# One engine for the sums of the Strassen projections, and swapped PSUM pools

## The chip, the cores and the metric

The kernel runs on one core of a Trainium2 chip. The metric is the device time of one execution in microseconds (us). The engines are TensorE (PE, with its weight loads PEld), VectorE (DVE), ScalarE (ACT), GpSimd (POOL) and SyncE (SP, which here issues most DMA transfers). Matrix products accumulate in PSUM, which is split into eight banks; everything else lies in SBUF.

## The reference, cut to what matters

```python
for layer in range(2):
    if layer == 0:
        h = rms_norm(x, norm_even)
        a_u, a_z, q, k, v, b_z = split(h @ w_in_even)
        ya = s5_branch(a_u, ...) * silu(a_z)
        yb = retention_branch(q, k, v, gn_gain) * silu(b_z)
        x = x + concatenate([ya, yb]) @ w_out_even      # (1024 x 2048) @ (2048 x 1024): stage E
    else:
        h = rms_norm(x, norm_odd)
        p = h @ w_in_odd                                # u, v, z of 2048 columns each
        y = spatial_gating(gelu(u), gelu(v), ...) * silu(z)
        x = x + y @ w_out_odd                           # (1024 x 2048) @ (2048 x 1024): stage O
return rms_norm(x, final_norm)
```

The sequence has 1024 positions, the model 1024 channels, and everything is float32.

## The kernel before, in words

**Numbers.** A float32 product is made of three products of a shorter format. `split` (lines 64 to 66) makes the high half of a tile with a cast on ACT (L65, `whi` for weights, `yhi` for activations) and the low half with a subtraction on DVE (L66, `wlo`, `ylo`). `mm3` (L102 to L104) then issues high by high, low by high and high by low into one PSUM bank.

**Projections.** Both output projections, E after the even layer and O after the odd one, run through `strassen_out`, a seven-product scheme (Strassen and Winograd) over 2x2 blocks. Products p0 to p6 follow one another. Each has four quarters c0 to c3 of its inner dimension, and each quarter is 24 matmuls: 4 row blocks, 2 slices, 3 products of `mm3`. Between the products stand sums of blocks, a quarter at a time and 128x1024 in size: of weights `s1` = a21 + a22 (L1330), `s2` = s1 - a11 (through `vsub`), a12 - s2 for p3 (L1308) and a11 - a21 for p5 (L1312); of activations `t1`, `t2`, `t3` (through `vsub`) and `t4` (L1342). `sums(n)` places them a fixed number of quarters behind the start. `prep` makes the operands of a quarter, `evac` (L1354) adds a finished bank into an SBUF tile, p2 takes the banks of p1 again, p3 goes on accumulating on p2's sums and p4 to p6 on p0's, so that such a product's first matmul in a bank waits for the eviction of what stands there. Raw weights arrive in two pools, `raw` (two buffers) and `wr` (five buffers), all loaded from SP's queue in a chain (`load`, L1241).

**Before E** stands the last step of the attention: its output `on` is normalised on DVE (L1148) and transposed on PE into `ps_ot` (L1158). **The v units** of the retention projections (`quads_sums`, L785; rotary products L903 to L909) have four 256-column blocks of weights and the sums s1 (L793), s2 (L794), a11 - a21 (L795) and a12 - s2 (L1025). The same `quads_sums` also serves sv2, a later stage of the odd layer.

**Order.** Each engine executes its instructions in order. That order is made by a scheduler that simulates the time line, from the dependences and the order of the code. `tc.issue_after(x)` adds an edge that keeps an instruction behind x; the list `lastv` holds the last DVE operation of the chain, and `vsub` uses it. In `run_e` the pools of four PSUM banks each are handed over as `psAs`; p0 takes `psAs[False]`, and p1 to p3 take the other one. Banks become free in the order in which their former users finish.

In the trace, tiles named slS2h and slS2l (E) or slT1h and slT1l (O) hold s1 and s2; slB... and slT... hold activations and their sums, and slC... the results.

Of the kernel before, what the change touches and what calls it, by code (L numbers as in the profile page):

```python
# [14 lines left out]
MUL, ADD, SUB = ALU.mult, ALU.add, ALU.subtract  # L15
# [10 lines left out]
def tile_hybrid_trunk(ctx: ExitStack, tc: tile.TileContext, A, out, dbg=None):  # L26
    nc = tc.nc
# [36 lines left out]
    def split(hi, lo, src, E=nc.vector):  # L64
        nc.scalar.copy(hi, src)  # L65
        return E.tensor_tensor(lo, src, hi.bitcast(F32), SUB)  # L66
# [206 lines left out]
    with tc.tile_pool(name="s5p", bufs=1, reuse_waits="tile") as pp:  # L273
# [72 lines left out]
        V = nc.vector  # L346
# [436 lines left out]
            a = vq[k] = uw.tile([128, 4, 256], F32, tag="a2", name=f"a2{k}", bufs=2)  # L783
            ld(out=a, in_=wcols(w, c0 + 256, 256, 4 * k, 4))

    def quads_sums():
        i = done[0]
        done[0] += 2
        a11, a12, a21, a22 = raws[i], raws[i + 1], vq[0], vq[1]
        s1 = uw.tile([128, 4, 256], F32, tag="s14", name="s1")  # L790
        s2 = uw.tile([128, 4, 256], F32, tag="s23", name="s2")
        P = nc.gpsimd
        P.tensor_tensor(s1, a21, a22, ADD)  # L793
        P.tensor_tensor(s2, s1, a11, SUB)  # L794
        P.tensor_tensor(a21, a11, a21, SUB)  # L795
        return a11, a12, s2, a21, a22, s1

# [163 lines left out]
    for n, (nm, h) in enumerate(seqB):  # L961
        nn = seqB[n + 1][0] if n + 1 < len(seqB) else None
        V = nc.vector
        if nm != "v":
            t0, t1, t2, t3 = nxt
            nxt = []
            if n < NEARLY:
                cA = cE[n]
            else:
                cA = c_pair("q")  # L970
                first_two(t0, cA)
            cB = c_pair("k")
            c11, c12, c21, c22 = cA[:, 0], cA[:, 1], cB[:, 0], cB[:, 1]
            if nn in ("q", "k", "z"):
                w_pair_raw()
                src = w_pair()
                nxt.append(w_pair_split(src[0]) if n + 1 >= NEARLY else None)
            if n == 0:
                with tc.issue_after(loads[max(raws)].ins):
                    load_tab()  # L980
                    load_tab()
            if nn is None:
                pre = {(0, 0): prefetch(0, 0)}
                yr = load_y()
            p6 = prodB(half(t1, 0), T2)
            V.tensor_tensor(c12, p6, c12, ADD)
            p7 = prodB(half(t1, 1), T3)
            V.tensor_tensor(c22, p7, c12, ADD)
            if nn in ("q", "k", "z"):
                nxt.append(w_pair_split(src[1]))  # L990
            p4 = prodB(t3, T4)
            V.tensor_tensor(c21, p4, c22, ADD)
            rot(nm, h, 0, c11, c21)
            if nn == "v":
                quads_raw(w_in, 4096 + seqB[n + 1][1] * 512)
                nxt.append(split4(raws[done[0]]))
            p5 = prodB(half(t2, 0), T1)
            V.tensor_tensor(c22, p5, c22, ADD)
            V.tensor_tensor(c12, p5, c12, ADD)
            if nn == "v":  # L1000
                nxt.append(split4(raws[done[0] + 1]))
            p3 = prodB(half(t2, 1), Be[1, 1])
            V.tensor_tensor(c12, p3, c12, ADD)
            if nn == "v":
                qs = quads_sums()
                qt = split4(qs[2])
            with tc.issue_after(loads["s4"].ins) if nn == "v" else ExitStack():
                rot(nm, h, 1, c12, c22)
            if nn in ("q", "k", "z"):
                nxt += [w_pair_split(o) for o in src[2:]]  # L1010
            elif nn is None:
                w_split(done[0])
        else:
            def keep(c, t, q):
                ld(out=vv_d[4 * t:4 * t + 4, :, h * 512 + q * 256:h * 512 + (q + 1) * 256].rearrange("c p d -> p c d"), in_=c)

            a11, a12, s2, s3, a22, s1 = qs
            c11, c12 = c_pair("q", (4, 256)), c_pair("q", (4, 256))
            p1 = prod4(PB, "p", Be[0, 0], nxt[0])
            post(c12, p1, None)  # L1020
            p2 = prod4(PB, "p", Be[1, 0], nxt[1])
            post(c11, p2, c12)
            keep(c11, 0, 0)
            c21, c22 = c_pair("k", (4, 256)), c_pair("k", (4, 256))
            nc.gpsimd.tensor_tensor(a12, a12, s2, SUB)  # L1025
            t2 = qt
            t3 = split4(s3)
            p6 = prod4(PB, "p", T2, t2)
            post(c12, p6, c12)
            t4 = split4(a22)  # L1030
            p7 = prod4(PB, "p", T3, t3)
            post(c22, p7, c12)
            t5 = split4(s1)
            p4 = prod4(PB, "p", T4, t4)
            post(c21, p4, c22)
            keep(c21, 0, 1)
            t6 = split4(a12)
            w_pair_raw()
            src = w_pair()
            nxt = [w_pair_split(src[0])]  # L1040
            p5 = prod4(PB, "p", T1, t5)
            post(c22, p5, c22)
            keep(c22, 1, 1)
            post(c12, p5, c12)
            nxt.append(w_pair_split(src[1]))
            p3 = prod4(PB, "p", Be[1, 1], t6)
            post(c12, p3, c12)
            keep(c12, 1, 0)
            nxt += [w_pair_split(o) for o in src[2:]]
        if 2 <= n < 6:  # L1050
            y_transpose(2 * n - 4)
            y_transpose(2 * n - 3)
# [181 lines left out]
    def strassen_out(w, wk, ysrc, yt, s2t, ct, xsrc, fin, ysl, nfirst, tmp=None, late=False, pre=None):  # L1234
# [29 lines left out]
        def wl(d, q, c, own=False):  # L1264
            a = op.tile([128, 2, 512], F32, tag="wr", name="wr", bufs=5) if own else wraw_p.tile([128, 2, 512], F32, tag="raw", name="raw")
            loads["wl"] = load(a, wcols(w, d * 512, 512, wk[8 * q + 2 * c], 2))
            return a

        def ws(src):
            hi = wspl_p.tile([128, 2, 512], F32R, tag="whi", name="whi")  # L1270
            lo = wspl_p.tile([128, 2, 512], F32R, tag="wlo", name="wlo")
            lastv[:] = [split(hi, lo, src)]
            return hi, lo

        lastv = []

        def ys(src):
            p, th, tl, n = ysl(yn[0], op)
            yn[0] += 1
            hi = p.tile([128, 2, 512], F32R, tag=th, name="yhi", bufs=n)  # L1280
            lo = p.tile([128, 2, 512], F32R, tag=tl, name="ylo", bufs=n)
            lastv[:] = [split(hi, lo, src)]
            return hi, lo

        V, P = nc.vector, nc.gpsimd
        op, yn = None, [0]
        C, ops = {}, {}
        first = []
# [12 lines left out]
        def prep(p, c):  # L1301
            if p < 2:
                return ws(wl(0, p, c)), ys(yf(p, 0, c))
            if p == 2 or p == 4:
                return ws(s2(c)), ys(yf(0, 0, c))
            if p == 3:
                a12 = wl(0, 1, c)
                P.tensor_tensor(a12, a12, s2(c), SUB)  # L1308
                return ws(a12), ys(yf(1, 1, c))
            if p == 5:  # L1310
                a11, a21 = wl(0, 0, c), wl(1, 0, c, True)
                P.tensor_tensor(a21, a11, a21, SUB)  # L1312
                return ws(a21), ys(yf(0, 1, c))
            return ws(wl(1, 1, c)), ys(yf(1, 0, c))

# [2 lines left out]
                if 0 <= n - o < 4:  # L1318
                    f(n - o)

        def vsub(o, a, b):
            with tc.issue_after(lastv[0].ins):
                lastv[:] = [V.tensor_tensor(o, a, b, SUB)]

        def sum_t1(c):
            vsub(yf(0, 0, c), yf(0, 1, c), yf(0, 0, c))

        def sum_s1(c):
            a21, a22 = wl(1, 0, c, True), wl(1, 1, c, True)
            P.tensor_tensor(s2(c), a21, a22, ADD)  # L1330

        def sum_s2(c):
            vsub(s2(c), s2(c), wl(0, 0, c, True))
# [5 lines left out]
            vsub(yf(0, 1, c), yf(1, 1, c), yf(0, 1, c))  # L1339

        def sum_t4(c):
            P.tensor_tensor(yf(1, 0, c), yf(1, 0, c), yf(0, 0, c), SUB)  # L1342

        def residual(n, t, d):
            C[n] = slot(*ct[n])
# [5 lines left out]

        def evac(p, i, ps):
            o = C[ADDS[p]][:, i]
            lastv[:] = [V.tensor_tensor(o, ps, o, ADD)]  # L1354
            if p == 1:
                pre(i, 0, o)
            if p == 4:
                pre(4 + i, 0, o)
            if p == 5:
                fin(4 + i, C["12"][:, i], o)  # L1360
            if p == 6:
                fin(i, C["11"][:, i], o)
# [65 lines left out]
    hpools["b01"] = b01.enter_context(tc.tile_pool(name="b01", bufs=1, side="right", reuse_waits="tile"))  # L1428
    with tc.tile_pool(name="oeB", bufs=1, reuse_waits="tile") as oeB, tc.tile_pool(name="psA0e", bufs=4, space=PS, reuse_waits="tile") as psA0, \
            tc.tile_pool(name="psA1e", bufs=4, space=PS, reuse_waits="tile") as psA1:  # L1430
        psAs = psA1, psA0
        run_e(oeB, psAs)
    oep.close()
    eb0.close()
# [27 lines left out]
                nc.vector.bn_stats(st[c0 + c][:, col // 256 + q, :], vt[:, c, q * 256:(q + 1) * 256])  # L1462
        ld(out=v_d[c0:c0 + n, :, col:col + vt.shape[2]].rearrange("c p d -> p c d"), in_=vt)

    with tc.tile_pool(name="sv", bufs=2, reuse_waits="tile") as vp, tc.tile_pool(name="psV", bufs=4, space=PS, reuse_waits="tile") as psV, \
            tc.tile_pool(name="psVa", bufs=4, space=PS, reuse_waits="tile") as psVa:
        wg = vp.tile([128, 4, 128], F32, name="wg", tag="cb0", bufs=1)
        ld(out=wg, in_=A["sgu_w_spatial"][0].rearrange("g t s -> t g s"))
        ld(out=bsb, in_=A["sgu_b_spatial"][0].rearrange("g t -> (g t)").partition_broadcast(128))
# [260 lines left out]
```

## Time and profile before

| | value |
|---|---|
| median of 3 runs | 1663.01 us (1661.65 to 1663.93) |
| the profiled run, its own time | 1663.19 us |
| its span, first to last instruction | 1661.0 us |
| mean granted clock of PE | 0.986 |
| PE busy | 1600.8 us (96%) |
| DVE busy | 1247.8 us (75%) |
| POOL busy | 680.3 us (41%) |
| ACT busy | 621.4 us (37%) |

The span runs 2.2 us shorter than the execution's time. "Clock" is the share of TensorE's full speed that was granted in a stretch. Stages, in us from the start of the span: S5 branch to 337, retention projections 337 to 613 (the v units from 432 and from 540), attention to 800, E 797 to 953, the odd layer's v and sv2 to 1143, u and z to 1470, O to the end.

### The profile page before, as it was taken

The numbers are of one execution on the slowest core, as the hardware profiler recorded it, in microseconds if no ns is written. First come the engines' busy times: TensorE is split into PE (matmuls) and PEld (weight loads), VectorE is DVE, ScalarE is ACT, GpSimd is POOL, SyncE is SP. The second block draws the span as 40 slices with busy tenths as digits, with TensorE's granted clock in tenths as the row PEclk, the third lists the DMA queues.
The fourth block names the chain that finished last, engine by engine and source line by source line (L and its number), as shares of the span: only waits on it lengthen the run. The fifth ranks groups of instructions, "written<-read, shape, count | busy, mean of one in ns | idle before, by whom it ended". The sixth has DMA issues, their size and how long they took to land.

```text
span 1661.0 us, 22787 instructions
## 1 busy us (share of the span) xinstructions
PE 1600.8 (96%) x8428; PEld 1358.3 (82%) x8428; DVE 1247.8 (75%) x1942; ACT 621.4 (37%) x803; POOL 680.3 (41%) x491
## 2 busy tenths in 40 slices
PE   7999999989899999999898999999999999999897
PEld 6888888868798988888776888998888888888676
DVE  7867777668876686565589676768998888857986
ACT  6523343443122232221333445333444444444244
POOL 4467777524545331000055023324444444424631
PEclk9999999999999999999999999999999999999899
DMA  8346777643545388654875243434233333359333
GB/s 226 89 118 146 181 164 177 170 131 95 171 153 177 100 296 309 223 184 145 296 274 165 90 141 117 149 102 127 92 111 103 101 97 101 97 202 337 121 99 127
DMA packets 256622, 261.79 MB, mean 158 GB/s; under 512 B 31712, under 2 KB 186112, under 8 KB 256512
## 3 DMA queue, kind: packets, MB, share of 16 engines
q1 hardware_dynamic: 246720, 240.42, 47.5%
q10 hardware_dynamic: 9792, 19.93, 3.2%
q8 instruction: 66, 1.08, 0.3%
q14 instruction: 44, 0.36, 0.1%
HBM read 186.90 MB, written 67.11 MB: 153 GB/s over the span
## 4 chain that ended last, share of the span: by engine, by line
PE 82%; DVE 8%; DMA 3%; issue 3%; POOL 2%; ACT 1%; SPq 1%; POOLq 0%; DVEq 0%; ACTq 0%
PE ps_uz L104 9%; PE ps_uz L103 9%; PE ps_uz L102 9%; PE ps_acc L103 4%; PE ps_acc L104 4%; PE ps_acc L102 4%; PE ps_vx L103 3%; PE ps_vx L104 3%; PE ps_vx L102 3%; PE ps_z L103 3%; PE ps_z L102 3%; PE ps_z L104 3%; DVE wlo L66 2%; PE ps_u L103 2%; PE ps_u L102 2%
## 5 line engine op out<-in xcount | busy, mean ns | idle before, releaser
L65 ACT CAST whi<-raw 128x1024 fp32r<-128x1024 f32 x110 | 115.5, 1051 | 242.5 <-PE ps_uz L103 50.0
L102 PE MATMUL ps_acc<-whi,yhi 128*128 128x512 f32 x448 | 176.3, 402 | 12.2 <-DVE slB11h L1354 7.0
L103 PE MATMUL ps_acc<-wlo,yhi 128*128 128x512 f32 x448 | 179.1, 400 | 7.0 <-DVE wlo L66 7.0
L104 PE MATMUL ps_acc<-whi,ylo 128*128 128x512 f32 x448 | 177.7, 398 | 0.0
L66 DVE TENSOR_TENSOR wlo<-raw,whi 128x1024 fp32r<-128x1024 f32 x94 | 137.0, 1458 | 43.7 <-ACT whi L65 43.0
L1622 DVE TENSOR_SCALAR vy<-vy,mu,rs 128x128 f32<-128x128 f32 x128 | 111.7, 939 | 5.0 <-DMA vy<-v_d 4.8
L102 PEld LDWEIGHTS ps_acc<-whi,yhi 128*128 128x128 f32 x448 | 86.3, 193 | 33.3 <-issue 7.6
L103 PEld LDWEIGHTS ps_acc<-wlo,yhi 128*128 128x128 f32 x448 | 85.8, 192 | 29.1 <-DVE wlo L66 10.2
L65 ACT CAST whi<-s 128x1024 fp32r<-128x1024 f32 x60 | 62.9, 1048 | 111.2 <-PE ps_uz L103 35.5
L104 PEld LDWEIGHTS ps_acc<-whi,ylo 128*128 128x128 f32 x448 | 85.7, 191 | 19.1
L103 PE MATMUL ps_z<-hl,whi 128*128 128x512 f32 (+1 forms) x248 | 94.9, 383 | 0.5 <-DVE hl L66 0.5
L102 PE MATMUL ps_z<-hh,whi 128*128 128x512 f32 (+1 forms) x248 | 94.4, 383 | 0.7 <-ACT hh L65 0.7
L104 PE MATMUL ps_z<-hh,wlo 128*128 128x512 f32 (+1 forms) x248 | 93.7, 378 | 0.0
L66 DVE TENSOR_TENSOR wlo<-s,whi 128x1024 fp32r<-128x1024 f32 x60 | 76.3, 1271 | 8.4 <-ACT whi L65 8.4
L736 POOL TENSOR_TENSOR s<-raw 128x512 f32<-128x512 f32 x25 | 33.7, 1349 | 118.4 <-DMA raw<-in_w_in_odd 83.5
L734 POOL TENSOR_TENSOR s<-raw 128x512 f32<-128x512 f32 x25 | 33.7, 1350 | 113.9 <-DMA raw<-in_w_in_even 58.0
L113 POOL TENSOR_TENSOR rs_r<-bva,nhalf 128x4 f32<-128x4 f32 x8 | 8.1, 1011 | 157.9 <-DVE bva L1145 157.9
L104 PE MATMUL ps_uz<-hh,wlo 128*128 128x512 f32 x144 | 57.1, 397 | 0.0
L103 PE MATMUL ps_uz<-hl,whi 128*128 128x512 f32 x144 | 57.0, 396 | 0.0
L102 PE MATMUL ps_uz<-hh,whi 128*128 128x512 f32 x144 | 56.5, 394 | 0.0
L113 POOL TENSOR_TENSOR rs_r<-rms_v,nhalf 128x1 f32<-128x1 f32 x24 | 15.9, 667 | 98.2 <-DVE rms_v L122 92.2
L66 DVE TENSOR_TENSOR whl<-raw,whl 128x512 fp32r<-128x512 f32 x25 | 31.5, 1261 | 30.9 <-ACT whl L65 30.9
(574 smaller groups left out, 5105.1 us busy)
## 6 DMA issues: line engine op xcount, KB each, us to landing
raw<-in_w_in_odd SPq DMA_DIRECT2D x50, 512.0 KB, 3.9
raw<-in_w_in_even SPq DMA_DIRECT2D x48, 512.0 KB, 4.6
raw<-in_w_out_even SPq DMA_DIRECT2D x20, 512.0 KB, 4.7
raw<-in_w_out_odd SPq DMA_DIRECT2D x20, 512.0 KB, 3.9
wr<-in_w_out_even SPq DMA_DIRECT2D x16, 512.0 KB, 6.8
vy<-v_d SPq DMA_DIRECT2D x32, 256.0 KB, 3.0
y_d<-c SPq DMA_DIRECT2D x32, 256.0 KB, 3.2
wr<-in_w_out_odd SPq DMA_DIRECT2D x16, 512.0 KB, 7.2
```

The source lines that it names most:

```text
L65: nc.scalar.copy(hi, src)
L66: return E.tensor_tensor(lo, src, hi.bitcast(F32), SUB)
L102: nc.tensor.matmul(ps, lh, rh, start=first, stop=False, skip_group_check=chain)
L103: nc.tensor.matmul(ps, lh, rl, start=False, stop=False, skip_group_check=chain)
L104: return nc.tensor.matmul(ps, ll, rh, start=False, stop=last, skip_group_check=chain)
L113: nc.gpsimd.tensor_tensor(r, v, nhalf[:, 0:n], ALU.pow)
L734: P.tensor_tensor(s14[:, 0:4], a21, a22, ADD)
L736: P.tensor_tensor(s23[:, 4:8], a11, a21, SUB)
L1622: V.tensor_scalar(vy[:, c, :], vy[:, c, :], mu2[:, cc:cc + 1], rs2[:, cc:cc + 1], op0=SUB, op1=MUL)
```

## The change

It has three parts. (1) In the retention's v units `quads_sums` gets VectorE for s1 and s2; the third sum and L1025 stay on GpSimd, and sv2's calls keep GpSimd for all. (2) In `strassen_out` the sums s1, a12 - s2, a11 - a21 and t4, 16 operations of 128x1024 in each out-projection, go from GpSimd to VectorE through `vsub`; a12 gets a buffer of the pool `wr` in place of `raw`; splits are chained with the sums through `vsplit`, and `evac` enters the chain only with a product's second bank. (3) The pools handed to `run_e` are swapped, and psV and psVa are created in swapped order.

```diff
-    def quads_sums():
+    def quads_sums(E=nc.gpsimd):
...
-        P.tensor_tensor(s1, a21, a22, ADD)
-        P.tensor_tensor(s2, s1, a11, SUB)
+        E.tensor_tensor(s1, a21, a22, ADD)
+        E.tensor_tensor(s2, s1, a11, SUB)
         P.tensor_tensor(a21, a11, a21, SUB)
...
             if nn == "v":
-                qs = quads_sums()
+                qs = quads_sums(V)
...
-            lastv[:] = [split(hi, lo, src)]
+            vsplit(hi, lo, src)
             return hi, lo

         lastv = []
+
+        def vsplit(hi, lo, src):
+            with tc.issue_after(lastv[0].ins) if op is not None and lastv else ExitStack():
+                lastv[:] = [split(hi, lo, src)]
...
-                a12 = wl(0, 1, c)
-                P.tensor_tensor(a12, a12, s2(c), SUB)
+                a12 = wl(0, 1, c, True)
+                vsub(a12, a12, s2(c))
...
-                P.tensor_tensor(a21, a11, a21, SUB)
+                vsub(a21, a11, a21)
...
-        def vsub(o, a, b):
+        def vsub(o, a, b, f=SUB):
             with tc.issue_after(lastv[0].ins):
-                lastv[:] = [V.tensor_tensor(o, a, b, SUB)]
+                lastv[:] = [V.tensor_tensor(o, a, b, f)]
...
-            P.tensor_tensor(s2(c), a21, a22, ADD)
+            vsub(s2(c), a21, a22, ADD)
...
-            P.tensor_tensor(yf(1, 0, c), yf(1, 0, c), yf(0, 0, c), SUB)
+            vsub(yf(1, 0, c), yf(1, 0, c), yf(0, 0, c))
...
-            lastv[:] = [V.tensor_tensor(o, ps, o, ADD)]
+            r = V.tensor_tensor(o, ps, o, ADD)
+            if i == 1:
+                lastv[:] = [r]
...
-        psAs = psA1, psA0
+        psAs = psA0, psA1
...
-    with ... psV = tc.tile_pool(name="psV", bufs=4, space=PS, ...), psVa = tc.tile_pool(name="psVa", bufs=4, space=PS, ...):
+    with ... psVa = tc.tile_pool(name="psVa", bufs=4, space=PS, ...), psV = tc.tile_pool(name="psV", bufs=4, space=PS, ...):
```

What this does to the order of the engines' instructions, at three places. The first is PE at the start of E, before:

```order
L1128 MATMUL ps_o<-vraw,sd 128x256
L1158 MATMUL ps_ot<-ident,on 128x128 [waits DVE_49,Activation_49]
L1158 MATMUL ps_ot<-ident,on 128x128 [waits PE_49]
L1158 MATMUL ps_ot<-ident,on 128x128 [waits DVE_49]
L1158 MATMUL ps_ot<-ident,on 128x128
L1158 MATMUL ps_ot<-ident,on 128x128 [waits DVE_49,Activation_49]
L1158 MATMUL ps_ot<-ident,on 128x128
L1158 MATMUL ps_ot<-ident,on 128x128 [waits DVE_49]
L1158 MATMUL ps_ot<-ident,on 128x128
L102 MATMUL ps_acc<-whi,yhi 128x512 [waits PE_49]
L103 MATMUL ps_acc<-wlo,yhi 128x512
```

In the changed kernel 37 matmuls of p0 follow the same ps_o; these are the last of them, the transposes, and how p0 goes on:

```order
L104 MATMUL ps_acc<-whi,ylo 128x512
L102 MATMUL ps_acc<-whi,yhi 128x512
L103 MATMUL ps_acc<-wlo,yhi 128x512
L104 MATMUL ps_acc<-whi,ylo 128x512
L102 MATMUL ps_acc<-whi,yhi 128x512
L1158 MATMUL ps_ot<-ident,on 128x128 [waits DVE_49] x2
L1158 MATMUL ps_ot<-ident,on 128x128
L1158 MATMUL ps_ot<-ident,on 128x128 [waits DVE_49] x2
L1158 MATMUL ps_ot<-ident,on 128x128 x3
L103 MATMUL ps_acc<-wlo,yhi 128x512
L104 MATMUL ps_acc<-whi,ylo 128x512
```

The first 37 matmuls of p0 have moved ahead of the eight transposes of the attention output. The second place is DVE in E, between the last split of p2 (`wlo<-slS2l`) and those of p3, before (p3's a12 - s2, `raw`, is made on POOL):

```order
L66 TENSOR_TENSOR wlo<-slS2l,whi 128x1024
L1323 TENSOR_TENSOR slB10h<-slB11h,slB10h 128x1024
L66 TENSOR_TENSOR ylo<-slB11h,yhi 128x1024 x2
L1354 TENSOR_TENSOR slC_7539<-ps_acc,slC_7539 128x512
L66 TENSOR_TENSOR wlo<-raw,whi 128x1024
L1323 TENSOR_TENSOR slS2l<-slS2l,wr 128x1024
L1354 TENSOR_TENSOR slC_7539<-ps_acc,slC_7539 128x512
L1323 TENSOR_TENSOR slB10l<-slB11l,slB10l 128x1024
L1354 TENSOR_TENSOR slC_7539<-ps_acc,slC_7539 128x512
L66 TENSOR_TENSOR wlo<-raw,whi 128x1024
L66 TENSOR_TENSOR ylo<-slB11l,yhi 128x1024
```

The same place on DVE in the changed kernel:

```order
L66 TENSOR_TENSOR wlo<-slS2l,whi 128x1024
L66 TENSOR_TENSOR ylo<-slB10l,yhi 128x1024
L1327 TENSOR_TENSOR slS2h<-slS2h,wr 128x1024
L1327 TENSOR_TENSOR slB10h<-slB11h,slB10h 128x1024
L1327 TENSOR_TENSOR wr<-wr,slS2h 128x1024
L66 TENSOR_TENSOR wlo<-wr,whi 128x1024
L66 TENSOR_TENSOR ylo<-slB11h,yhi 128x1024
L1358 TENSOR_TENSOR slC_7539<-ps_acc,slC_7539 128x512 x2
L1327 TENSOR_TENSOR slS2l<-slS2l,wr 128x1024
L1327 TENSOR_TENSOR slB10h<-slB11h,slB10h 128x1024
L1327 TENSOR_TENSOR wr<-wr,slS2h 128x1024
L1358 TENSOR_TENSOR slC_7539<-ps_acc,slC_7539 128x512 x2
```

For each quarter of p3 the sums, a12 - s2 among them (`wr<-wr,slS2h`), now stand on DVE just ahead of the quarter's two splits, and the evictions of p2 come in pairs. The third place is DVE in the first v unit, before:

```order
L992 TENSOR_TENSOR ck<-ps_uz,ck 128x512
L998 TENSOR_TENSOR ck<-ps_uz,ck 128x512
L999 TENSOR_TENSOR cq<-ps_uz,cq 128x512
L1003 TENSOR_TENSOR cq<-ps_uz,cq 128x512
L903 TENSOR_TENSOR ro<-cq,rtab 128x512
L904 TENSOR_TENSOR ro<-ck,rtab 128x512
L905 TENSOR_TENSOR cq<-cq,rtab 128x512
L906 TENSOR_TENSOR ck<-ck,rtab 128x512
L66 TENSOR_TENSOR wlo<-s_4208,whi 128x1024
```

and in the changed kernel:

```order
L992 TENSOR_TENSOR ck<-ps_uz,ck 128x512
L793 TENSOR_TENSOR s_4207<-a_4166,a_4168 128x1024
L998 TENSOR_TENSOR ck<-ps_uz,ck 128x512
L999 TENSOR_TENSOR cq<-ps_uz,cq 128x512
L794 TENSOR_TENSOR s_4208<-s_4207,raw 128x1024
L903 TENSOR_TENSOR ro<-cq,rtab 128x512
L904 TENSOR_TENSOR ro<-ck,rtab 128x512
L1003 TENSOR_TENSOR cq<-ps_uz,cq 128x512
L905 TENSOR_TENSOR cq<-cq,rtab 128x512
L66 TENSOR_TENSOR wlo<-s_4208,whi 128x1024
```

The sums L793 and L794 have come in between the evictions, and one eviction and one rotary product (L1003, L906) have moved back by one or two places.

## Rows read from the trace of the kernel before

**Rows 1.** Page, part 1: busy us, share of the span, instructions.

```profile
PE 1600.8 (96%) x8428; PEld 1358.3 (82%) x8428; DVE 1247.8 (75%) x1942; ACT 621.4 (37%) x803; POOL 680.3 (41%) x491
```

**Rows 2.** Stretches: us, busy PE PEld DVE ACT POOL, clock, DMA share, GB/s.

```profile
432.00:470.00 38.00, 32.98 (x267) 32.62 (x265) 31.60 (x32) 6.22 (x7) 23.20 (x12) 0.91 0.50 167
...
785.00:800.00 15.00, 9.93 (x43) 8.42 (x43) 10.51 (x26) 4.52 (x6) 1.01 (x1) 0.89 0.84 275
800.00:953.00 153.00, 143.14 (x607) 115.86 (x606) 121.35 (x118) 57.61 (x73) 50.16 (x20) 0.97 0.60 204
...
1530.00:1600.00 70.00, 60.59 (x246) 47.59 (x245) 69.96 (x42) 22.15 (x25) 43.67 (x16) 0.93 0.50 166
```

**Rows 3.** Waits of PE by stage (E, O, v unit, sv2): us, times, longest.

```profile
PE ps_acc L102 <- ACT whi L65: 5.3, 1, 5.3
PE ps_ot L1158 <- DVE on L1148: 5.1, 1, 5.1
PE ps_acc L103 <- DVE wlo L66: 4.6, 3, 1.8
...
PE ps_acc L102 <- DVE slB11h L1354: 7.0, 1, 7.0
PE ps_acc L103 <- DVE wlo L66: 2.5, 3, 1.4
...
PE ps_vx L103 <- DVE wlo L66: 5.0, 1, 5.0
...
PE ps_vx L102 <- DVE vt L1499: 0.8, 1, 0.8
```

**Rows 4.** Stretches just behind waits of PE, columns as in rows 2.

```profile
448.00:456.00 8.00, 6.88 (x41) 6.89 (x42) 8.00 (x9) 0.00 (x0) 4.34 (x2) 0.64 0.80 262
796.00:800.00 4.00, 4.00 (x17) 3.45 (x16) 4.00 (x6) 1.05 (x1) 0.00 (x0) 0.68 0.53 154
866.00:872.00 6.00, 6.00 (x20) 4.33 (x18) 6.00 (x6) 0.63 (x2) 2.38 (x1) 0.72 0.59 175
884.00:892.00 8.00, 6.74 (x18) 4.87 (x19) 8.00 (x4) 2.63 (x3) 5.34 (x2) 0.58 0.44 137
1558.00:1566.00 8.00, 8.00 (x25) 6.32 (x25) 8.00 (x7) 0.00 (x0) 5.88 (x3) 0.68 0.63 199
```

**Rows 5.** Timeline of DVE: start us, length us, instruction, idle before.

```profile
441.68 2.89 DVE L904 TENSOR_TENSOR ro<-ck,rtab 128x512 f32<-128x512 f32 x1
...
883.82 6.60 DVE L66 TENSOR_TENSOR wlo<-raw,whi 128x1024 fp32r<-128x1024 f32 x2
...
909.28 1.21 DVE L1323 TENSOR_TENSOR slB01l<-slB11l,slB01l 128x1024 f32<-128x1024 f32 x1
910.42 1.21 DVE L66 TENSOR_TENSOR wlo<-slS2l,whi 128x1024 fp32r<-128x1024 f32 x1
```

**Rows 6.** Timeline of POOL at the same places.

```profile
441.16 2.86 POOL L795 TENSOR_TENSOR a<-raw,a 128x1024 f32<-128x1024 f32 x1
...
882.67 3.36 POOL L1342 TENSOR_TENSOR slB00h<-slB00h,slB10h 128x1024 f32<-128x1024 f32 x1
886.00 3.34 POOL L1342 TENSOR_TENSOR slB00l<-slB00l,slB10l 128x1024 f32<-128x1024 f32 x1
```

**Rows 7.** Stretches of DVE alone around p3: us, busy (count), clock, DMA, GB/s.

```profile
850.00:892.00 42.00, 37.18 (x25) 0.88 0.53 180
1540.00:1590.00 50.00, 49.96 (x29) 0.90 0.46 142
```

**Rows 8.** Stretch 808 to 856, in E, columns as in rows 2.

```profile
808.00:856.00 48.00, 48.00 (x213) 39.58 (x212) 38.27 (x31) 19.12 (x24) 12.46 (x5) 1.00 0.99 354
```

**Rows 9.** Timeline of DVE before p3 of E.

```profile
853.14 1.21 DVE L66 TENSOR_TENSOR wlo<-slS2l,whi 128x1024 fp32r<-128x1024 f32 x1
...
859.89 0.68 DVE L1354 TENSOR_TENSOR slC<-ps_acc,slC 128x512 f32<-128x512 f32 x1
```

**Rows 10.** Page, part 5: casts of weights on ACT, busy us, mean ns.

```profile
L65 ACT CAST whi<-raw 128x1024 fp32r<-128x1024 f32 x110 | 115.5, 1051 | 242.5 <-PE ps_uz L103 50.0
```

More of the change, by code (lines that the diff above doesn't have):

```diff
@@ L1281, in ys @@
             lo = p.tile([128, 2, 512], F32R, tag=tl, name="ylo", bufs=n)
-            lastv[:] = [split(hi, lo, src)]
+            vsplit(hi, lo, src)
             return hi, lo
-        V, P = nc.vector, nc.gpsimd
+        V = nc.vector
         op, yn = None, [0]
@@ L1463, in keep_v @@
         ld(out=v_d[c0:c0 + n, :, col:col + vt.shape[2]].rearrange("c p d -> p c d"), in_=vt)
-    with tc.tile_pool(name="sv", bufs=2, reuse_waits="tile") as vp, tc.tile_pool(name="psV", bufs=4, space=PS, reuse_waits="tile") as psV, \
-            tc.tile_pool(name="psVa", bufs=4, space=PS, reuse_waits="tile") as psVa:
+    with tc.tile_pool(name="sv", bufs=2, reuse_waits="tile") as vp, tc.tile_pool(name="psVa", bufs=4, space=PS, reuse_waits="tile") as psVa, \
+            tc.tile_pool(name="psV", bufs=4, space=PS, reuse_waits="tile") as psV:
         wg = vp.tile([128, 4, 128], F32, name="wg", tag="cb0", bufs=1)
```

## The prediction

> **What bounds the kernel now.** I read the busy times first: TensorE (PE) works 96% of the span, VectorE (DVE) 75%, GpSimd (POOL) 41% [rows 1]. So the time is PE's work plus PE's idle stretches plus what a halved clock costs, and the busy shares of the other engines say little. The table by stage shows where PE is not full: four stages that the change touches have PE busy below the stage's length and a granted clock below 1.00, the first v unit (432 to 470 us), the last attention step before the even out-projection (785 to 800), the out-projection E (800 to 953) and the middle of the odd out-projection O (1530 to 1600) [rows 2]. The waits of PE then name the late engine: in E 5.3 us for a cast of weights and three waits of 4.6 us together for the low halves of splits on DVE, 5.1 us before E for the attention output, in O 7.0 us for an eviction on DVE and 2.5 us for three splits, in the v unit 5.0 us for one split, and 0.8 us for a PSUM bank in sv2 [rows 3]. Third come the clocks: after such a wait PE runs with a granted clock between 0.58 and 0.72 for 4 to 8 us [rows 4], the mean of stretches at the full level of 2.4 GHz and at 1.2 GHz.
>
> Why are DVE's splits late? The timeline of DVE beside that of POOL answers it. Two splits of 128x1024 took 6.60 us at 883.82 [rows 5], while POOL ran two subtractions of 3.36 and 3.34 us over the same time [rows 6]; at 909.28, with POOL idle, DVE starts such operations 1.14 us apart [rows 5]. Over 850 to 892 DVE was busy 37.18 us with 25 instructions, four of them evictions of 0.68 us, which leaves 1.64 us for each of 21 SBUF operations; over 1540 to 1590 it is (49.96 - 7 x 0.68) / 22 = 2.05 us [rows 7]. DVE is late in E and O because POOL's sums lengthen its own work.
>
> **The change, part by part.** The profiled run took 1663.19 us, which is the median of the runs (1663.01) within 0.2 us, so I count from 1663.2.
>
> **Start of E.** Product p0 now accumulates in the banks that the attention scores and outputs have left, so PE has 37 of its matmuls ahead of the eight transposes ps_ot that wait for DVE. Operands of the first two quarters are split long before. At some 0.225 us each (48 us for 213 rows [rows 8]) 37 matmuls are 8.3 us, more than the wait of 5.1 us [rows 3]. PE also no longer idles into a low clock: 4.0 us at 0.68 lose 4.0 x 0.32 = 1.3 us [rows 4]. Gain 6.4 us; the bounds are 0 (the lead is swallowed later) and 6.4, and I take 6.4, because the operands are there.
>
> **Product p3 of E.** The waits are 5.3 + 4.6 = 9.9 us [rows 3]. The clock costs 6.0 x 0.28 = 1.7 us and 6.74 x 0.42 = 2.8 us [rows 4], so 14.4 us can be had. What remains afterwards is DVE's own length. Sixteen sums come onto DVE in each out-projection, 16 x 1.14 = 18.2 us, and POOL's 16 leave. In the new order the block from the second sum s2 to the last split of p3 has 19 SBUF operations, 4 evictions and 3 places where DVE stands for ACT's cast of a tile it has just made: 19 x 1.14 + 4 x 0.68 + 3 x 1.05 = 27.5 us [rows 5, 9, 10]. In that time PE has four quarters of 24 matmuls at 0.225 us, 21.6 us, plus its lead: the split for p2's last quarter ended at 854.35, and PE began that quarter near 857.9 (the eviction of its first bank is at 859.89), so 3.5 us of lead [rows 8, 9]. The shortfall is 27.5 - 25.1 = 2.4 us; if the earlier start has eaten the lead it is 5.9. I take the middle, 4.1, and for the clock the present proportion, 4.5 / 9.9 of it, 1.8. Of 14.4 us 5.9 stay: gain 8.5, bounds 5.8 (5.9 us of wait and 2.7 of clock stay) and 14.4.
>
> **Product p3 of O.** Waits 7.0 + 2.5 = 9.5 us [rows 3], clock 8.0 x 0.32 = 2.6 us [rows 4], together 12.1. The same block of DVE work stands there, so the same 5.9 stay: gain 6.2. Eight operations on the final gain stay on POOL in O; where they meet the block it gets longer. Bounds 0 and 12.1.
>
> **First v unit.** The wait is 5.0 us, the clock costs 6.88 x 0.36 = 2.5 us [rows 3, 4], 7.5 in all. Two sums move from POOL to DVE and stand between four evictions that read PSUM. But POOL keeps two sums and the rotary sums, so DVE's rotary products still meet them: one that took 2.89 us ran beside POOL's 2.86 us [rows 5, 6]. If none met POOL, the split would end before PE wants it (gain 7.5). If two still do, 2 x (2.89 - 0.68) = 4.4 us come back on DVE (0.68 as an eviction of that size takes [rows 9]), the wait is about 3.0 us and the gain 3.0. I take 3.8, nearer the second, since POOL's four operations are all still there. The second v unit shows no wait, so its sums cost nothing while DVE stays ahead of PE there.
>
> The Trainium skill speaks to this, "SBUF — State Buffer", section "SBUF: two separate sides": DVE and GpSimd share a port pair that is held exclusively for a whole instruction, and a DVE operation with two SBUF inputs blocks against a GpSimd operation that reads SBUF. The trace agrees (6.60 us for two operations instead of 2.3). By that rule moving only two of the sums speaks against the v part, since every sum left on POOL still stops DVE: it would be worth 3.0 us, where the 1.14 us of the undisturbed rows would make it 7.5.
>
> **The rest.** sv2's first bank wait of 0.8 us [rows 3] goes with the swap of the two pools (bounds 0 and 0.8). The own buffer for a12 lets its loads start earlier at no cost, hidden behind PE. The chain of splits and sums adds no instruction; what it can add is waiting, below.
>
> Sum: 6.4 + 8.5 + 6.2 + 3.8 + 0.8 = 25.7 us, 1663.2 - 25.7 = 1637.5, **1638 us**.
>
> **The rivals.** *Everything comes back.* If the lead holds and DVE keeps ahead, all of 6.4 + 14.4 + 12.1 + 7.5 + 0.8 = 41.2 us go: 1622. For it: undisturbed DVE needs only 2.4 us more than PE gives. Against it: the casts that DVE now waits for one by one.
>
> *Head of the line.* DVE executes in order, and with the chain a sum that waits for its weights holds every split and eviction behind it; on POOL such a wait held nothing of DVE. From 808 to 856 the DMA engines are 0.99 busy [rows 8], so loads can hardly come earlier than today even if PE starts E sooner: the 6.4 us of the start return as a wait at p2 or p3. In O the sum s1 of the second quarter now stands behind two evictions of p1, so the buffers of its weights come free some 4 us later, and so do the loads behind them on SP's queue: 4 us of wait, 5.8 with the clock's share. The gain is 25.7 - 6.4 - 5.8 = 13.5 us: 1650.
>
> *Slower: DVE's operations do not shorten.* The forecast rests on 1.14 us an operation. Should the 1.64 and 2.05 us of today [rows 7] come from something other than POOL, with DVE taking 16 operations more, then the shortfall at p3 is 19 d - 19.2 us with d the length of one: it reaches today's 9.9 us at d = 1.53. With today's means it is 12.0 us in E and 19.8 in O, 2.1 and 10.3 us more than now, 18 with the clock's share; less 6.4 and 0.8 the kernel is 10.8 us slower: 1674. Against it: the 1.14 us beside an idle POOL [rows 5].
>
> *Nothing moves.* The waits are replaced by others of the same sum (a wait at p2 for weights, a later one at p5): 1661 to 1666.
>
> **How the numbers follow.** Forecast (1630 to 1645) 0.55, head of the line 0.20, everything 0.12, no change 0.06, slower 0.07. The range of 8 in 10 runs from the 1622 of the best case to a little past the 1650 of the head of the line, 1652. A difference under 0.2%, 3.3 us, is what a measurement of this kernel cannot tell from no change; faster by more has 0.87, within 0.06, slower 0.07.
>
> **What would show it.** Right: DVE's SBUF operations in E and O start about 1.14 us apart throughout, POOL nearly empty there; PE's rows show ps_acc ahead of ps_ot with no gap at 790 to 797; at p3 one or two waits for a split of 2 to 6 us together in each out-projection; the v unit's wait at about half. Wrong: DVE operations of 2 us and more with POOL idle (the slower rival), or DVE idle at a sum with a DMA of weights as the releaser while PE waits (head of the line). The largest uncertainty is the lead of p3, since 3.5 us of it is one reading.

## The result, and the profile after

The changed kernel takes **1635.7 us** (median of 4 runs, 1634.3 to 1636.6) against 1662.8 us (4 runs), a ratio of 0.9836 with a 95% interval of 0.9819 to 0.9853: 27 us faster, at 1638 forecast. The profiled execution has a span of 1632.5 us (1634.34 us in all) and a mean granted clock of 0.995.

Busy times of the whole span, which answer to [rows 1]:

```profile
PE 1592.7 (98%) x8428; PEld 1350.8 (83%) x8428; DVE 1236.3 (76%) x1978; ACT 621.8 (38%) x803; POOL 581.9 (36%) x455
```

PE worked 8 us less for the same 8428 rows (less time at the low clock), and the span fell by 28.5: the other 20 us were waits. POOL lost 98 us of busy time, DVE has 36 more rows and yet 11 us less. Next the stages, which answer to [rows 2] (us, busy time of PE, PEld, DVE, ACT, POOL, granted clock, DMA share, GB/s):

```profile
432.00:470.00 38.00, 35.44 (x307) 35.03 (x306) 31.12 (x34) 6.75 (x8) 20.49 (x11) 1.00 0.54 178
...
785.00:800.00 15.00, 15.00 (x72) 12.34 (x71) 9.77 (x23) 6.43 (x8) 1.01 (x1) 1.00 0.88 294
800.00:953.00 153.00, 149.89 (x676) 122.86 (x675) 130.22 (x174) 66.62 (x92) 10.20 (x9) 1.00 0.62 212
...
1500.00:1575.00 75.00, 72.75 (x300) 56.31 (x299) 66.45 (x60) 28.02 (x33) 8.55 (x5) 0.98 0.47 161
```

PE fills 785 to 800 now, and the clock stays at 1.00 in the first three; only O keeps a dip, to 0.98. POOL's 50.16 us in E have become 10.20. What PE still waits for, in the v unit, in E and in O (us in total, times, longest), against [rows 3]:

```profile
PE ps_vx L103 <- DVE wlo L66: 2.6, 1, 2.6
...
PE ps_acc L102 <- DVE slC L1358: 2.4, 2, 1.5
PE ps_acc L102 <- ACT yhi L65: 0.6, 1, 0.6
...
PE ps_acc L102 <- DVE slT4h L1358: 2.0, 1, 2.0
PE ps_acc L103 <- DVE wlo L66: 1.6, 1, 1.6
PE ps_acc L104 <- DVE ylo L66: 0.9, 1, 0.9
PE ps_acc L102 <- ACT whi L65: 0.5, 1, 0.5
```

E keeps 3.0 us of 15.0 (with the start), O 5.0 of 9.5, the v unit 2.6 of 5.0. The wait for the attention output and the one for sv2's bank have no row any more. PE's timeline at the start of E, and DVE's row that the transposes wait for:

```profile
785.36 0.59 PE L1128 MATMUL ps_o<-vraw,sd 128*128 128x256 f32 x2
785.61 0.58 PE L102 MATMUL ps_acc<-whi,yhi 128*128 128x512 f32 x1
...
790.47 1.39 DVE L1148 TENSOR_SCALAR on<-on,bmv,rs_r 128x256 f32<-128x256 f32 x4
```

p0 begins at 785.61, behind the last ps_o without a gap, and works while DVE normalises `on` until 791.86. In p3 of E, DVE's timeline (start, length) reads, against [rows 5]:

```profile
853.27 1.22 DVE L1327 TENSOR_TENSOR slS2l<-slS2l,wr 128x1024 f32<-128x1024 f32 x1
854.40 1.22 DVE L1327 TENSOR_TENSOR slB10h<-slB11h,slB10h 128x1024 f32<-128x1024 f32 x1
855.54 1.22 DVE L1327 TENSOR_TENSOR wr<-wr,slS2h 128x1024 f32<-128x1024 f32 x1
856.67 1.29 DVE L1358 TENSOR_TENSOR slC<-ps_acc,slC 128x512 f32<-128x512 f32 x2
857.93 1.23 DVE L66 TENSOR_TENSOR wlo<-wr,whi 128x1024 fp32r<-128x1024 f32 x1
859.07 1.22 DVE L66 TENSOR_TENSOR ylo<-slB11h,yhi 128x1024 fp32r<-128x1024 f32 x1
```

Sum, sum, a12 - s2, two evictions, then the quarter's two splits. The operations of 128x1024 take 1.22 us and start 1.14 us apart, as beside an idle POOL, and all of E reads so.

Where the 28.5 us of span went can be read from when PE issues the same matmul in both traces (E's last products stand among the first of the odd layer, so they end later than the 953 us given for the stage):

| PE issues | before | after | gain so far | of this stage |
|---|---|---|---|---|
| last product of the retention (v units) | 574.2 | 569.7 | 4.5 | 4.5 |
| last product of E | 969.4 | 946.7 | 22.7 | 18.2 |
| first product of O | 1482.3 | 1457.3 | 25.0 | 2.3 |
| last product of O | 1651.9 | 1622.2 | 29.7 | 4.7 |
| end of the span | 1661.0 | 1632.5 | 28.5 | -1.2 |

The later experiments ran beside other runs of the kernel before (medians of 1663.9 to 1664.6 us), so they are compared by their ratios to these: 0.001 is 1.7 us.

### The profile page after: what moved, and what is told of

The parts are those of the page before. It is cut to its first block, busy times and chain, and to the rows that moved or that the text cites. A ratio compares the mean times of both kernels' runs of the same rounds, so it can differ in the third digit from the quotient of the medians.

```text
span 1632.5 us, 22726 instructions
## 1 busy us (share of the span) xinstructions
PE 1592.7 (98%) x8428; PEld 1350.8 (83%) x8428; DVE 1236.3 (76%) x1978; ACT 621.8 (38%) x803; POOL 581.9 (36%) x455
## 4 chain that ended last, share of the span: by engine, by line
PE 89%; DVE 5%; DMA 2%; issue 1%; ACT 1%; POOL 1%; SPq 0%; POOLq 0%; DVEq 0%; ACTq 0%
PE ps_uz L102 9%; PE ps_uz L103 9%; PE ps_uz L104 9%; PE ps_acc L103 5%; PE ps_acc L102 5%; PE ps_acc L104 5%; PE ps_vx L103 3%; PE ps_vx L104 3%; PE ps_z L103 3%; PE ps_vx L102 3%; PE ps_z L102 3%; PE ps_z L104 3%; PE ps_u L102 2%; PE ps_u L104 2%; PE ps_gl L103 2%; PE ps_u L103 2%
## 5 line engine op out<-in xcount | busy, mean ns | idle before, releaser
L65 ACT CAST whi<-raw 128x1024 fp32r<-128x1024 f32 x102 | 107.2, 1051 | 210.4 <-PE ps_uz L103 47.3
L102 PE MATMUL ps_acc<-whi,yhi 128*128 128x512 f32 x448 | 161.7, 395 | 5.5 <-DVE slC L1358 2.4
L103 PE MATMUL ps_acc<-wlo,yhi 128*128 128x512 f32 x448 | 162.7, 395 | 1.6 <-DVE wlo L66 1.6
L104 PE MATMUL ps_acc<-whi,ylo 128*128 128x512 f32 x448 | 162.0, 395 | 0.9 <-DVE ylo L66 0.9
L66 DVE TENSOR_TENSOR wlo<-raw,whi 128x1024 fp32r<-128x1024 f32 x86 | 115.8, 1347 | 42.0 <-ACT whi L65 37.9
```

The source lines that it names most:

```text
L102: nc.tensor.matmul(ps, lh, rh, start=first, stop=False, skip_group_check=chain)
L103: nc.tensor.matmul(ps, lh, rl, start=False, stop=False, skip_group_check=chain)
L104: return nc.tensor.matmul(ps, ll, rh, start=False, stop=last, skip_group_check=chain)
```

## The experiments

My theory was the prediction's: the banks free PE at the start of E, and POOL's sums lengthen DVE's operations until p3's splits are late. The rivals: the lead is swallowed, the order of DVE's queue did it and not the engine, or the own buffer of a12.

**The banks alone.** The kernel before, with

```diff
-        psAs = psA1, psA0
+        psAs = psA0, psA1
...
-    with tc.tile_pool(name="sv", bufs=2, reuse_waits="tile") as vp, tc.tile_pool(name="psV", bufs=4, space=PS, reuse_waits="tile") as psV, \
-            tc.tile_pool(name="psVa", bufs=4, space=PS, reuse_waits="tile") as psVa:
+    with tc.tile_pool(name="sv", bufs=2, reuse_waits="tile") as vp, tc.tile_pool(name="psVa", bufs=4, space=PS, reuse_waits="tile") as psVa, \
+            tc.tile_pool(name="psV", bufs=4, space=PS, reuse_waits="tile") as psV:
```

> The kernel before, with only the two swaps of PSUM pools. Theory (banks let PE work through the wait of the attention output): PE goes on with ps_acc at about 790.5 instead of 797.05, no gap there, gain 6.4 + 0.8 us, time about 1656. Rival (the lead is swallowed, because p3's operands come from POOL and from a saturated DMA stretch no earlier than now): the waits of p3 grow by as much, time 1661 to 1664.

Measured: ratio 0.9944 [0.9923, 0.9964], 9 us. PE went on into p0 without a gap. E took 171.7 us from its first matmul to its last, where the kernel before took 179.0 from the point at which PE stopped: 7.3 us. The waits of PE in E, from the trace of this run:

```profile
PE ps_acc L103 <- DVE wlo L66: 9.8, 2, 8.7
PE ps_acc L102 <- ACT whi L65: 1.1, 1, 1.1
```

They sum to 10.9 us, and 0.8 us more for an eviction, against 9.9 before. So about 1.8 us of the lead came back as waits, the rest stayed. The rival is out. (Only E is compared here: this execution ended the v units 3.9 us later than the kernel before, on the same code.)

**The banks taken back,** the same lines the other way round in the changed kernel.

> The changed kernel, with the two swaps of PSUM pools taken back. Theory: the wait for the attention output returns (5.1 us and 1.3 us of clock), less what the smaller lead saved at p3, time 1641 to 1643. Rival (p3 is short of DVE time anyway, the lead is worth nothing): time 1636 to 1637, with the waits of p3 smaller by as much as the start's wait is larger.

Measured: 0.9873 [0.9851, 0.9896], 6 us slower than the changed kernel's 0.9836; the 5.07 us in front of the transposes are back. The theory holds here too: the part is worth about what it was priced at, with and without the others.

**The sums back on POOL,** a11 - a21 and t4 in the same way as the two shown, everything else as changed:

```diff
+        def psub(o, a, b, f=SUB):
+            nc.gpsimd.tensor_tensor(o, a, b, f)
...
-                vsub(a12, a12, s2(c))
+                psub(a12, a12, s2(c))
...
-            vsub(s2(c), a21, a22, ADD)
+            psub(s2(c), a21, a22, ADD)
```

> The changed kernel with the same chain of splits, the same buffers and banks, but the 16 sums (s1, a12 - s2, a11 - a21, t4) of each out-projection on GpSimd as before, outside the chain. Theory (POOL's instructions lengthen DVE's): DVE has fewer instructions in E and O, yet those beside POOL's sums take 2 to 3.4 us instead of 1.2; the waits of p3 return, 8 to 12 us in E and 3 to 6 in O, time 1648 to 1654. Rival (the order did it: splits in order of use, evictions in pairs): DVE is relieved of 18 us in each out-projection and the time is 1630 to 1637.

Measured: 0.996 [0.9946, 0.9973], worse than the theory said: PE's waits are 10.5 us in E and 11.5 in O. E took 173.2 us (161.1 in the changed kernel) and O 175.3 us (164.9; 169.6 in the kernel before, and 171.2 in the run of the banks alone, with the same code there). The order alone, with POOL's sums, brings nothing in E and costs in O. In O PE now waits

```profile
PE ps_acc L104 <- DVE ylo L66: 6.3, 4, 2.6
PE ps_acc L102 <- DVE slB11h L1361: 4.2, 1, 4.2
```

for activations' low halves and for an eviction. One of these waits, with the two splits of p3 ahead of it on DVE and POOL's rows beside them:

```profile
1548.81 3.39 DVE L66 TENSOR_TENSOR wlo<-wr,whi 128x1024 fp32r<-128x1024 f32 x1
1552.12 3.37 DVE L66 TENSOR_TENSOR ylo<-slT3h,yhi 128x1024 fp32r<-128x1024 f32 x1
...
1547.83 3.28 POOL L1330 TENSOR_TENSOR wr<-wr,slT1l 128x1024 f32<-128x1024 f32 x1 [3.50 <-DMA slB11l<-x_d]
1551.08 3.33 POOL L1330 TENSOR_TENSOR slB10h<-slB10h,slB00h 128x1024 f32<-128x1024 f32 x1
...
1555.55 0.80 PE L104 MATMUL ps_acc<-whi,ylo 128*128 128x512 f32 x1 [2.57 <-DVE ylo L66]
```

DVE waited for none of POOL's sums: its rows show no idle time from 1516 to 1581, nor in E from 830 to 909. It was late because its operations took up to 3.4 us beside POOL's, at p3 itself.

**The chain taken out,** with the sums on VectorE:

```diff
-            with tc.issue_after(lastv[0].ins) if op is not None and lastv else ExitStack():
-                lastv[:] = [split(hi, lo, src)]
+            lastv[:] = [split(hi, lo, src)]
...
-            if i == 1:
-                lastv[:] = [r]
+            lastv[:] = [r]
```

> The changed kernel without the chain of splits (splits free of edges, every eviction in the chain as before); the sums stay on VectorE. Theory (the engine matters, the order little): 1635 to 1640. Rival (the order of use is what carries p3): the splits of p3 come late again behind sums of later quarters, time 1645 to 1652.

Measured: 0.9904 [0.9883, 0.9924], 11 us slower than the changed kernel. The theory is wrong here: in this trace 7.0 us of E and the whole gain of O hang on the chain (E 168.1 us, O 170.9). DVE's timeline in p3 of E, and PE's row that waits for it:

```profile
856.84 1.22 DVE L1326 TENSOR_TENSOR wr<-wr,slS2h 128x1024 f32<-128x1024 f32 x1
...
861.38 2.35 DVE L1326 TENSOR_TENSOR wr<-wr,slS2l 128x1024 f32<-128x1024 f32 x2
863.65 1.22 DVE L66 TENSOR_TENSOR ylo<-slB10h,yhi 128x1024 fp32r<-128x1024 f32 x1
864.79 3.49 DVE L66 TENSOR_TENSOR wlo<-wr,whi 128x1024 fp32r<-128x1024 f32 x3
...
866.06 0.80 PE L103 MATMUL ps_acc<-wlo,yhi 128*128 128x512 f32 x1 [5.68 <-DVE wlo L66]
```

Every operation of 128x1024 starts 1.14 us behind the one before. The first row is the sum a12 - s2 that PE's next quarter needs. Behind it stand six operations for later quarters (three are left out above), two of them a12 - s2 for the third and fourth (861.38) and one a split for p4 (863.65), and only then, at 864.79, the split of the first; in the changed kernel it stands at 857.93. PE waits 5.68 us.

**Every eviction in the chain,** the splits still chained:

```diff
-            if i == 1:
-                lastv[:] = [r]
+            lastv[:] = [r]
```

> The changed kernel, with every eviction in the chain and not only a product's second one; the splits stay chained. Theory (the chained splits carry the 13 us that the run without the chain lost, the pairing of evictions little): ratio 0.9836 to 0.985. Rival (the pairing carries them): ratio 0.988 to 0.991.

Measured: 0.9865 [0.9846, 0.9885], 5 us slower, between the theory and the rival, and its interval just touches the changed kernel's. (The 13 us named there are E and O of the trace without the chain; by time that run lost 11.) In this trace E took 164.5 us and O 169.1, against 161.1 and 164.9 in the changed kernel, so the pairing carries a part of what the chain gives. Why is not shown; a likely reason is that a chained eviction holds what follows until PE has finished that bank. The two parts were not taken apart the other way round.

**Idle additions on POOL.** In the changed kernel, behind each of the 32 moved sums:

```diff
+            if not dz:
+                dz.append(op.tile([128, 768], F32, tag="dz", name="dz", bufs=1))
+                nc.gpsimd.memset(dz[0], 0.0)
+            with tc.issue_after(lastv[0].ins):
+                nc.gpsimd.tensor_tensor(dz[0], dz[0], dz[0], ADD)
```

> The changed kernel, and behind each of the 32 sums that came to VectorE GpSimd adds a scratch tile of 128x768 to itself; nobody reads or waits for it. VectorE's order stays as in the changed kernel. Theory (a POOL instruction that reads SBUF holds up DVE's): DVE's operations beside them take 2 to 3 us in place of 1.2, waits of PE return in E and O, 8 to 20 us more than the changed kernel, ratio 0.988 to 0.996. Rival (the gain came from the order of the sums and from sums no longer queueing on a slow engine): DVE's operations stay at 1.2 us, ratio 0.9836 within 0.002.

Measured: 0.9902 [0.9885, 0.9919], 11 us slower, with DVE's order unchanged. POOL, which waits for nobody here, ran its additions in one go at the start of E and of O. POOL's row, and DVE's beside and behind it:

```profile
791.01 34.39 POOL L1337 TENSOR_TENSOR dz<-dz 128x768 f32<-128x768 f32 x16
791.19 6.08 DVE L1148 TENSOR_SCALAR on<-on,bmv,rs_r 128x256 f32<-128x256 f32 x4
821.59 2.48 DVE L66 TENSOR_TENSOR ylo<-slB00l,yhi 128x1024 fp32r<-128x1024 f32 x1
826.40 1.21 DVE L66 TENSOR_TENSOR wlo<-raw,whi 128x1024 fp32r<-128x1024 f32 x1
```

POOL added from 791.01 to 825.40, beside p0 and p1. The operation of 128x1024 that DVE began at 821.59 took 2.48 us, the first one after the additions 1.21. Of the 11 us, E took 5.4 and O 6.5 (by PE's first and last matmul). So POOL's instructions cost PE this much without touching a tile of the kernel: contention is shown apart from order here, and at p3 by the rows of the run with the sums back on POOL. The Trainium skill's lock ("SBUF — State Buffer", section "SBUF: two separate sides") says the same, and goes further: with two SBUF inputs DVE is held up only by a GpSimd operation that reads SBUF.

**Idle sets on POOL,** at the same places, once and then three times over:

```diff
-                nc.gpsimd.tensor_tensor(dz[0], dz[0], dz[0], ADD)
+                nc.gpsimd.memset(dz[0], 0.0)
```

> As the run with the scratch additions, but GpSimd writes a constant into the scratch tile, so it reads nothing from SBUF. Theory (it is POOL's reading beside DVE's two inputs that collides): DVE stays at 1.2 us, ratio 0.9836 within 0.002. Rival (any POOL instruction holds up DVE): DVE operations of 1.6 us and more beside them, ratio 0.986 or more.

> As the run in which GpSimd sets a scratch tile, three times over, so that its sets last as long (some 36 us in E) as the scratch additions did. Theory (reading is what collides with VectorE's operations on two SBUF tiles): those stay at 1.2 us beside the sets and the ratio is 0.983 to 0.986; only one-input operations of VectorE such as L1148 may be longer. Rival (the sets did no harm because they were short): VectorE's two-input operations beside them take 1.6 us or more, ratio 0.988 or more.

Measured: 0.9839 [0.9814, 0.9864] and 0.9839 [0.9821, 0.9856], the changed kernel's time. From the run with three sets, POOL's row and DVE's beside it:

```profile
791.95 38.37 POOL L1337 MEMSET dz<- 128x768 f32 x48
792.15 3.16 DVE L1148 TENSOR_SCALAR on<-on,bmv,rs_r 128x256 f32<-128x256 f32 x4
819.53 1.23 DVE L1327 TENSOR_TENSOR slB10h<-slB01h,slB10h 128x1024 f32<-128x1024 f32 x1 [1.09 <-DMA slB01h<-yab_d]
822.62 1.22 DVE L66 TENSOR_TENSOR wlo<-raw,whi 128x1024 fp32r<-128x1024 f32 x1 [1.86 <-ACT whi L65]
```

POOL set the tile from 791.95 to 830.32, longer than it had added, and the sum and the split at 819.53 and 822.62 took 1.23 and 1.22 us. It is the reading that collides; the trace agrees with that sentence of the Trainium skill.

**The v unit undone and carried further.** `qs = quads_sums()` in place of `quads_sums(V)`, and, the other way, all four sums of a v unit on VectorE:

```diff
-        P.tensor_tensor(a21, a11, a21, SUB)
+        E.tensor_tensor(a21, a11, a21, SUB)
...
-            nc.gpsimd.tensor_tensor(a12, a12, s2, SUB)
+            nc.vector.tensor_tensor(a12, a12, s2, SUB)
```

> The changed kernel with the v units' sums s1 and s2 back on GpSimd. Theory: the wait of 5.0 us in the first v unit returns for the 2.6 us of now, and with it the low clock behind it (2.5 us): 4.9 us more than the changed kernel, ratio to the kernel before about 0.9865. Rival (the v unit's wait is hidden, since the stages behind it have slack): 0.9836 as the changed kernel.

> The changed kernel, with all four sums of each v unit on VectorE (a11 - a21 and a12 - s2 too). Theory: the two rotary products that take 2.9 us beside them fall to 0.7, which gives 4.4 us back for 2.3 us of new work ahead of or behind the split, the wait of 2.6 us shrinks to 0 to 1.5 us: ratio 0.982 to 0.983. Rival (the two new sums stand ahead of the split that PE waits for): wait of 2.6 to 5 us, ratio 0.9836 to 0.985.

Measured: undone 0.9845 [0.9826, 0.9863], all four 0.9817 [0.98, 0.9834]. Undoing the part cost 1.5 us by time where the theory had 4.9: its 0.9865 lies just outside the interval and the rival's 0.9836 inside. All four came out just below the theory's range. Both intervals overlap with the changed kernel's, so the times decide little, and the traces say more. From the first to the last product of the v units PE took 141.3 us in the kernel before, 140.7 undone, 136.6 in the changed kernel and 134.7 with all four; but the eight other runs with the changed code there spread from 136.6 to 140.5. Undone, the wait is 5.02 us again. In the changed kernel DVE's rows before the split, and POOL's beside them, are

```profile
437.57 1.21 DVE L794 TENSOR_TENSOR s<-s,raw 128x1024 f32<-128x1024 f32 x1
438.70 2.90 DVE L903 TENSOR_TENSOR ro<-cq,rtab 128x512 f32<-128x512 f32 x1
441.52 2.89 DVE L904 TENSOR_TENSOR ro<-ck,rtab 128x512 f32<-128x512 f32 x1
...
445.53 1.21 DVE L66 TENSOR_TENSOR wlo<-s,whi 128x1024 fp32r<-128x1024 f32 x1
...
437.57 3.48 POOL L795 TENSOR_TENSOR a<-raw,a 128x1024 f32<-128x1024 f32 x1
441.01 2.85 POOL L1025 TENSOR_TENSOR raw<-raw,s 128x1024 f32<-128x1024 f32 x1
```

The two rotary products from 438.70 take 2.90 and 2.89 us beside POOL's two remaining sums. With these on VectorE they take 0.68 each, the split starts at 441.75, and the wait of PE in the v unit is

```profile
PE ps_vx L103 <- DVE wlo L66: 0.4, 1, 0.4
```

**a12 in its old buffers,** `a12 = wl(0, 1, c)`:

> The changed kernel, with a12 in the two buffers of raw again. Theory (the own buffer only keeps loads early that PE does not wait for): 0 to 2 us more than the changed kernel, ratio 0.9835 to 0.985. Rival (with the chain, a sum that waits for its load holds all splits behind it): VectorE stands idle at a12 - s2 with a DMA of raw as releaser, p3's waits grow by 4 us or more in each out-projection, ratio 0.988 or more.

Measured: 0.9835 [0.982, 0.9851]. With the sums on VectorE the own buffer is worth nothing that can be measured; VectorE never stood for a load of raw at p3 of E. The own buffer alone, in the kernel before, was not run.

**More for VectorE.** All four sums of the v units, and in O the products with the final gain:

```diff
-        nc.gpsimd.tensor_tensor(c, c, fg[0][:, 0:512], MUL)
+        nc.vector.tensor_tensor(c, c, fg[0][:, 0:512], MUL)
```

> The run with all sums of the v units on VectorE, and in O also the eight products with the final gain (L1595) on VectorE. Theory: the five VectorE operations that take 1.9 to 2.3 us beside them fall to 1.2, 5 us come back for 2.4 us of new work ahead of p3, and the waits of O's p3 (0.5 + 1.7 us and 1.2 us of clock) shrink to 0 to 1 us: ratio 0.979 to 0.981. Rival (each product waits for ScalarE's square of the same tile and holds up the splits behind it): ratio 0.982 to 0.985.

Measured: 0.9802 [0.9786, 0.9818], 1631.4 us against 1664.6 beside it: 33 us below the kernel before, some 6 below the changed one (the intervals just miss each other). In the changed kernel DVE's rows around p1's end in O, and POOL's, are

```profile
1502.05 2.31 DVE L1327 TENSOR_TENSOR slT1h<-wr 128x1024 f32<-128x1024 f32 x1
1505.48 1.22 DVE L66 TENSOR_TENSOR wlo<-slT1h,whi 128x1024 fp32r<-128x1024 f32 x1
1506.62 2.31 DVE L66 TENSOR_TENSOR ylo<-slB00h,yhi 128x1024 fp32r<-128x1024 f32 x1
1508.86 2.31 DVE L1327 TENSOR_TENSOR slT1l<-wr 128x1024 f32<-128x1024 f32 x1
...
1499.75 3.52 POOL L1595 TENSOR_TENSOR slT4l<-slT4l,fgain 128x512 f32<-128x512 f32 x2 [37.14 <-ACT sq L1586]
1506.14 3.94 POOL L1595 TENSOR_TENSOR slT4l<-slT4l,fgain 128x512 f32<-128x512 f32 x2 [2.87 <-ACT sq L1586]
```

Beside POOL's products with the gain 2.31 us stand for 1.2. With these on VectorE O takes 162.0 us (164.9). But not as I said: p3's wait did not shrink. PE's waits of O for splits of weights are

```profile
PE ps_acc L103 <- DVE wlo L66: 3.0, 1, 3.0
```

one of 3.0 us at p3 (0.3 us more for an activation's low half), where two had been 2.1 together; what went were the 2.8 us of waits later in O, at p5. The ratio fell into the theory's range by another way than the theory's.

## Why the prediction was right, and where it was not

**What bounds the kernel.** Right: v unit, E and O gave 27.4 us (2.3 more came between them, 1.2 were lost at the end), and the lengthened operations were POOL's doing, as the additions and the sets show. That the total came within 3 us is in part luck: E gave 3.3 us more than it was priced at, O 2.7 less.

**Start of E, 6.4 us.** Right in mechanism and size: 9 us for the banks alone (sv2's 0.8 among them), 6 us when they alone are taken back.

**p3 of E, 8.5 us.** Start and p3 were put at 14.9 us together and gave 18.2. The block of DVE work was counted rightly: p3's last split ended at 872.98 and the block began at 843.98, 29.0 us for the 27.5 said, 1.3 of the difference because the first cast came late (DVE stood 2.32 us for it). The term that was mis-sized is what remains: 5.9 us forecast, 3.0 found. The two waits left at p3 are 0.6 and 1.5 us where I had put 4.1, a third of 0.9 us came later, and the clock stayed at 1.00 behind them where I had charged 1.8 us. The lead was still there: PE began p2's last quarter at 846.68, 3.8 us behind the end of its split of weights at 842.93, for the 3.5 us that I had read. And neither wait is for a split, as I had said: the first is for a cast of activations on ACT, the second for an eviction of p2, which stands behind three sums on DVE.

One thing I read past in the kernel before. Its longest wait in E, 5.28 us, was for a cast, and that cast began as POOL ended its own sums a12 - s2, which had stood 5.5 us for a load of `raw`:

```profile
876.49 6.22 POOL L1308 TENSOR_TENSOR raw<-raw,slS2l 128x1024 f32<-128x1024 f32 x2 [5.53 <-DMA raw<-in_w_out_even]
...
882.74 1.99 ACT L65 CAST whi<-raw 128x1024 fp32r<-128x1024 f32 x2 [4.68 <-POOL raw L1308]
```

So POOL's lateness was on this path itself, beside what it did to DVE's operations, and no run parts the two in the kernel before. In the run with POOL's sums, the own buffers and the chain this wait is gone, DVE's operations are as long as before, and E is no shorter (173.2 us).

**The chain priced at nothing.** This is the step that failed, though the total hides it. I wrote that what the chain can add is waiting, and gave p3's whole gain to the faster operations. Without the chain, with all operations at 1.14 us, 11 us are lost; with the chain and POOL's sums, all that p3 gained in E is lost and O becomes slower than before. Neither does it alone: a fast queue in the wrong order brings the needed split as late as a slow one, and in a strict order every lengthened operation delays the split that PE needs. My sum was near since I took the block from the new order, which already contained the chain.

**p3 of O, 6.2 us.** 4.7 came, less 1.2 at the very end: 3.5. The failed step is "the same 5.9 stay": I had mentioned the products with the final gain that stay on POOL, and charged nothing. They lengthen four operations by 0.7 to 1.1 us ahead of p3 and three more, to 2.31 us each, at p5; taking them off POOL made O 2.9 us shorter, by the waits at p5 and not those at p3. The 1.2 us of the tail are not explained by any row that I found.

**First v unit, 3.8 us.** 4.5 came in the profiled execution; the other runs with the same code there, and the 1.5 us that undoing it cost, leave open how much of it the change made. The wait left is 2.6 us for 2.5 forecast, and it was made as said, by two rotary products beside POOL's sums. What differed is the clock: 1.2 us were charged (the 3.7 left of 7.5, in the proportion of before), and this profile shows 1.00 there. Other runs with the same code there and the same 2.6 us of wait show 0.96 for 432 to 470 (the three with idle work on POOL) or 1.00 (the one with the old banks), so this term varies from one execution to the next.

**The rest, 0.8 us.** 2.3 came between E and O; sv2's bank wait is gone, and a wait for an eviction there fell from 2.3 to 1.7 us, which leaves 0.9 us open.

**The rivals.** The head of the line did not come true: at p3 DVE stands for no load in the changed kernel, and the run with chain and POOL's sums shows no idle DVE there either. "Everything comes back" did not: 10.6 us of waits are left (2.6 in the v unit, 3.0 in E, 5.0 in O). "DVE's operations do not shorten" is ruled out by the 1.14 us.

## What to carry to other kernels

When an engine's operations are longer in one stage than elsewhere, look at what runs on VectorE and GpSimd at the same moments before giving either more work: here 16 operations more on VectorE made it finish sooner. Price the order of a queue as a term of its own, with the place at which the needed instruction stands, because the engine and the order together gave 16 us in E and O behind E's start, where the engine alone gave 3 and the order alone lost 6.5 (by PE's first and last matmul in one execution each; the same code took 169.6 and 171.2 us for O in two, so 1 or 2 us of each are noise). What stays on the other engine has to be charged for as well: the eight products left on GpSimd, and two sums of a v unit, were the next 6 us.

## What the hardware showed that I had not expected

GpSimd's sets of a constant did not slow a VectorE operation with two SBUF inputs at all (1.22 us beside them), but they did slow one with a single tensor as input: the four normalisations L1148, 1.39 us together in the changed kernel, took 3.16 us beside the sets and 6.08 us beside the additions (the first rows of DVE in the two fences above). So which GpSimd instruction collided depended, in these runs, on the form of VectorE's.
